# Taking each feed-forward down projection one chunk later

## The chip, the cores and the metric

The kernel runs on one core of one Trainium2 chip. The metric is the device time of one execution in microseconds (us). Three executions of the kernel before took 2207.88, 2215.27 and 2216.32 us; their median, 2215.27 us, is the time before.

Five engines work side by side and wait for each other through semaphores: PE (TensorE, matmuls, with PEld for its weight loads), ACT (ScalarE), DVE (VectorE), POOL (GpSimd, used here mostly to issue DMAs) and SP (SyncE, which issues the other DMAs). Each engine takes its own instructions in order.

## The reference, cut to what matters

A four-layer model on 256 tokens of width 1024, all in 32-bit floats. Each layer is feed-forward block, mixer, feed-forward block, and each of the three is followed by a layer norm over a scaled residual. The mixers are a state-space block (layers 0 and 3) and two kinds of attention (layers 1 and 2). So there are eight feed-forward blocks, all of the same form:

```python
def swiglu(x, w_gate, w_up, w_down):
    return (jax.nn.silu(x @ w_gate) * (x @ w_up)) @ w_down

ff = swiglu(h, ffn_w_gate[layer, 0], ffn_w_up[layer, 0], ffn_w_down[layer, 0])
h = layer_norm(DEEPNORM_ALPHA * h + MACARON_WEIGHT * ff, ln_g[layer, 0], ln_b[layer, 0])
```

The hidden width is 2816, which is 11 chunks of 256 columns.

## The kernel before

**Streams.** The 256 tokens are two tiles of 128 tokens, t = 0 and t = 1. Each is a Python generator (`stream`, and inside it `ffn`, `ssm` or `attn`) that yields whenever it needs the next piece of weights. The loop at the end of `build` advances stream 0 to piece s and then stream 1 to piece s - 2 (`LAG` = 2), so the two streams use the same weights two pieces apart and their matmuls alternate on PE.

**Weights.** All weights are cut on the host into pieces of 128 x 2048 floats (1 MB) in the order in which `ffn`, `ssm` and `attn` ask for them; `pack_ffn` sets that order for a feed-forward block, 33 pieces: 22 of gate and up columns (two per chunk) and 11 of down rows (one per chunk). `load` fetches a piece by a DMA on SP into one of three `raw` buffers, and then splits it in four quarters into a rounded high part `wh` (ACT, L123) and the rest `wl` (DVE, L124), with five buffers of each. `advance` loads two pieces ahead of stream 0 (`PF` = 2); a buffer comes free when stream 1 has used it. Every product is three matmuls (`mm3`, L148 to L150): high by high, high activations by low weights, low activations by high weights. A piece is 12 matmuls of 128 x 512 in either stream.

**A chunk.** `proj512` makes gate and up of chunk c, 256 columns each, in one PSUM bank `gu` from two pieces (24 matmuls). ACT takes the SiLU of the gate half (L269), DVE multiplies it by the up half (L271). The down projection (`down`, into the two banks `acc`) needs the product transposed and split into `ah` and `al`. The transpose does not use PE: `turn_begin` transposes 32 x 32 blocks on DVE (`tb`, L240), POOL writes the result to DRAM (`turn`, L242) and issues four DMAs that read it back in the turned layout (`aT`, L246). `turn_end` splits `aT` into `ah` on ACT and `al` on DVE (both lines 123 and 124, as for weights). The ACT half is held to its place in program order. Three `aT` buffers are there.

**The order before.** In `ffn`, chunk c's gate-up pieces are followed by the down piece of chunk c - 1, whose `turn_end` stands between the two halves of chunk c:

```python
for c in range(NC_F + 1):
    ...
    if half and c:
        acts[c - 1] = turn_end(turns.pop(c - 1))
    ...
    if c > 0:
        w = yield
        down(st, *acts.pop(c - 1), w, c == 1, c == NC_F)
```

In pieces: gate-up 0 (pieces 0 and 1), gate-up 1 (2 and 3), down 0 (4), gate-up 2 (5 and 6), down 1 (7), and so on. Chunk 10, the last, does not go through DRAM: its product is transposed on PE by `act_split` at high priority, after down 9 has been written. The order inside each engine's queue is finally set by the framework's scheduler, which follows the program but may pull work of one stream ahead of the other's.

Of the kernel before, what the change touches and what calls it, by code (L numbers as in the profile page):

```python
# [7 lines left out]
F32 = mybir.dt.float32  # L8
FR = mybir.dt.float32r
BF = mybir.dt.bfloat16  # L10
AF = mybir.ActivationFunctionType
# [9 lines left out]
NC_F = DFF // 256  # L21
# [24 lines left out]
def mixer_of(layer):  # L46
    return ("ssm", "fox", "moba")[layer % 3], layer // 3


def build(tc, x, wst, ln_g, ln_b, sm_dt, sm_rows, sm_conv, sm_nw, fx_f, fx_b, out, plan=None):  # L50
    nc = tc.nc
# [4 lines left out]
    spool = ctx.enter_context(tc.tile_pool(name="s", bufs=2))  # L56
# [13 lines left out]
    def G():  # L70
        return ps_g.tile([128, 512], F32, name="gu")
# [4 lines left out]
    def tmp(cols, tag, bufs, dt=F32):  # L76
        return spool.tile([128, cols], dt, name=tag, tag=tag, bufs=bufs)
# [44 lines left out]
    def split(raw, wh, wl):  # L122
        a = nc.scalar.activation(wh, raw, AF.Copy)  # L123
        return a, nc.vector.tensor_sub(wl, raw, wh.bitcast(F32))  # L124
# [22 lines left out]
    def mm3(o, xh, xl, wh, wl, start, stop):  # L147
        nc.tensor.matmul(o, xh, wh, start=start, stop=False)  # L148
        nc.tensor.matmul(o, xh, wl, start=False, stop=False)  # L149
        nc.tensor.matmul(o, xl, wh, start=False, stop=stop)  # L150
# [4 lines left out]
    def transposes(src, n):  # L155
        tp = T()
        for j in range(n):
            nc.tensor.transpose(tp[:, j * 128:(j + 1) * 128], src[:, j * 128:(j + 1) * 128], ident)  # L158
        return tp
# [43 lines left out]
    def down(st, ah, al, w, first, last):  # L203
        wh, wl = w
        if first:
            st.acc = [ps_a.tile([128, 512], F32, name=f"acc{n}") for n in range(2)]
        for m in range(4):
            kk, n = (m % 2, m // 2) if last else (m // 2, m % 2)
            o = kk * 1024 + n * 512
            mm3(st.acc[n], ah[:, kk], al[:, kk], wh[:, o:o + 512], wl[:, o:o + 512],  # L210
                first and kk == 0, last and kk == 1)

    def proj512(st, ps, half, w):
        wh, wl = w
        for kk in range(4):
            k = half * 4 + kk
            mm3(ps, st.xh[:, k], st.xl[:, k], wh[:, kk * 512:(kk + 1) * 512], wl[:, kk * 512:(kk + 1) * 512],
                k == 0, k == KT - 1)
# [7 lines left out]
    def act_split(src, n):  # L226
        tp = transposes(src, n)
        pairs = []
        for m in range(0, n, 2):
            ah = spool.tile([128, 2, 128], FR, name="ah", bufs=5)  # L230
            al = spool.tile([128, 2, 128], FR, name="al", bufs=5)
            split(tp[:, m * 128:(m + 2) * 128].rearrange("p (a b) -> p a b", a=2), ah, al)
            pairs.append((ah, al))
        return pairs

    def turn_begin(a, n):


        b = spool.tile([128, 4, n, 32], F32, name="tb", bufs=2)
        nc.vector.transpose(b.rearrange("p q k t -> p (q k t)"), a.rearrange("p (k q j) -> p q k j", k=n, q=4))  # L240
        dr = dpool.tile([128, 128 * n], F32, name="turn", bufs=4)
        nc.gpsimd.dma_start(dr, b.rearrange("p q k t -> p (q k t)"))  # L242
        aT = spool.tile([128, 4, n, 32], F32, name="aT", bufs=3)
        dv = dr.rearrange("(i f) (q c) -> q f i c", i=4, q=4)
        for q in range(4):
            nc.gpsimd.dma_start(aT[32 * q:32 * q + 32].rearrange("p i k t -> p i (k t)"), dv[q])  # L246
        return aT

    def turn_end(aT):
        ah = spool.tile([128, 2, 128], FR, name="ah", bufs=5)  # L250
        al = spool.tile([128, 2, 128], FR, name="al", bufs=5)
        v4 = lambda v: v.rearrange("p k (i t) -> p k i t", i=4)
        ins = split(aT.rearrange("p i k t -> p k i t"), v4(ah), v4(al))
        tc.keep_in_program_order(ins[0])
        return ah, al

    def ffn(st, hook):
        acts, turns = {}, {}
        for c in range(NC_F + 1):
            if c < NC_F:  # L260
                gu = G()
                for half in range(2):
                    w = yield
                    if half and c:
                        acts[c - 1] = turn_end(turns.pop(c - 1))
                    proj512(st, gu, half, w)
                with tc.high_priority() if c == NC_F - 1 else nullcontext():
                    sg = tmp(256, "t1", 5)
                    nc.scalar.activation(sg, gu[:, :256], AF.Silu)  # L269
                    a = tmp(256, "t1", 5)  # L270
                    nc.vector.tensor_mul(a, sg, gu[:, 256:])  # L271
                    if c < NC_F - 1:
                        turns[c] = turn_begin(a, 2)
            if c == 4 and hook is not None:
                hook()
            if c > 0:
                w = yield
                down(st, *acts.pop(c - 1), w, c == 1, c == NC_F)
            if c == NC_F - 1:
                with tc.high_priority():  # L280
                    acts[c] = act_split(a, 2)[0]

    def small():
        return tmp(32, "sm", 16)
# [457 lines left out]
    def stream(st):  # L742
        init(st)
        yield
        to_T(st, st.h)
        for n, (kind, l, li) in enumerate(plan):
            w = yield
            if n:
                with tc.high_priority():
                    to_T(st, st.h)  # L750
            if kind == "ffn":
                hook = None
                if st.t == 0 and n + 1 < len(plan) and plan[n + 1][0] == "mix":
                    mk, j = mixer_of(plan[n + 1][1])
                    hook = {"ssm": lambda j=j: ssm_small(j), "fox": lambda j=j: fox_small(j), "moba": consts}[mk]
                body = ffn(st, hook)
                c = 0.5 / ALPHA
            else:
                mk, j = mixer_of(l)
                body = ssm(st, j) if mk == "ssm" else attn(st, mk, j)  # L760
                c = 1.0 / ALPHA
            next(body)
            while True:
                try:
                    body.send(w)
                except StopIteration:
                    break
                w = yield
            layer_norm(st, c, li, n == len(plan) - 1)
            if st.t == 1 and n + 1 < len(plan):  # L770
                ln_weights(plan[n + 1][2])
# [23 lines left out]
    for kind, l, li in plan:  # L795
        n = 3 * NC_F if kind == "ffn" else 28 if mixer_of(l)[0] == "ssm" else 16
# [13 lines left out]
def rows2(a):  # L810

    n = a.shape[0] // 256
    return a.reshape(n, 2, 128, D).transpose(0, 2, 1, 3).reshape(n, 128, 2048)


def cols512(a):

    return list(a.reshape(2, 4, 128, 512).transpose(0, 2, 1, 3).reshape(2, 128, 2048))
# [6 lines left out]
def pack_ffn(g, u, d):  # L825
    P = []
    dn = rows2(d)
    for c in range(NC_F):
        sl = slice(c * 256, c * 256 + 256)
        P += cols512(np.concatenate([g[:, sl], u[:, sl]], axis=1))  # L830
        if c:
            P.append(dn[c - 1])
    P.append(dn[NC_F - 1])
    return P


def pack_ssm(w_in, w_out):
# [34 lines left out]
def layout(I, plan=None):  # L872
# [6 lines left out]
    for kind, l, li in plan:  # L879
        if kind == "ffn":  # L880
            h = 0 if li % 3 == 0 else 1
            P += pack_ffn(I["ffn_w_gate"][l, h], I["ffn_w_up"][l, h], I["ffn_w_down"][l, h])
            continue
        mk, j = mixer_of(l)
        if mk == "ssm":
            P += pack_ssm(I["ssm_w_in"][j], I["ssm_w_out"][j])
        else:
            P += pack_att(I[mk + "_w_in"][j], I[mk + "_w_out"][j])
# [39 lines left out]
```

## Time and profile before

| | |
|---|---|
| profiled execution, its own time | 2211.85 us |
| its span, first to last instruction | 2210.1 us |
| PE busy | 2142.6 us, 97% of the span |
| DVE busy | 1487.4 us, 67% |
| ACT busy | 1126.8 us, 51% |
| POOL busy | 478.2 us, 22% |
| DMA | 438.82 MB, mean 199 GB/s |
| granted TensorE clock, mean | 0.989 |
| feed-forward matmuls, `gu` of 512 columns | 3 x 1536, about 600 us each third |
| `acc` matmuls (feed-forward and mixers) | 3 x 896, about 359 us each third |

Times in the rows are microseconds from the start of the span unless they are marked ns. A row that ends with "[4.83 <-ACT ah L123]" says that the engine was idle for 4.83 us before that instruction and that the `ah` split on ACT, line 123, ended the idle time. Matmuls are pipelined, so their durations overlap; what counts is the distance from one start to the next. In a table of stretches each engine has its busy time and, in brackets, the number of its instructions that touch the stretch; PEclk is the mean clock that was granted to TensorE, 1.00 for full.

### The profile page before, as it was taken

How to read it: one execution, taken by the hardware profiler on the slowest of the kernel's cores; microseconds unless marked ns; L12 is line 12 of the kernel's file. 1: busy time of each engine (PE TensorE's matmuls, PEld its weight loads, DVE VectorE, ACT ScalarE, POOL GpSimd, SP SyncE). 2: the span in 40 equal slices, each digit the busy share in tenths (PEclk: the TensorE clock that was granted, in tenths of full speed). 3: DMA queues.
4: the chain of work that ended last, by engine and by line, in shares of the span. 5: the costliest groups of instructions: out<-in, count | busy, mean ns of one | idle time of the engine just before them, and what ended most of it. 6: DMA issues, size and time to landing. Idle time of an engine off the chain costs nothing.

```text
span 2210.1 us, 29948 instructions
## 1 busy us (share of the span) xinstructions
PE 2142.6 (97%) x10370; PEld 1779.5 (81%) x10370; DVE 1487.4 (67%) x2959; ACT 1126.8 (51%) x2314; POOL 478.2 (22%) x862
## 2 busy tenths in 40 slices
PE   8999999999999999999999999999999999999998
PEld 6888878788878888878878888878878888787887
DVE  5667998765756574656565674655566578998565
ACT  5444776444444445544444455544445447664442
POOL 2331000233133200033223310033323310002232
PEclk9999999999999999999999999999999999999999
DMA  8766554677666743466667764467656765455763
GB/s 290 226 222 200 186 176 154 205 226 223 206 216 224 226 154 115 148 209 225 219 205 226 225 201 133 134 196 228 222 194 226 235 191 191 164 177 194 221 225 104
DMA packets 225928, 438.82 MB, mean 199 GB/s; under 512 B 20464, under 2 KB 20976, under 8 KB 225776
## 3 DMA queue, kind: packets, MB, share of 16 engines
q1 hardware_dynamic: 197616, 394.92, 53.7%
q0 software_dynamic: 28160, 41.99, 6.7%
q8 instruction: 81, 1.33, 0.2%
q14 instruction: 71, 0.58, 0.1%
HBM read 414.74 MB, written 22.09 MB: 198 GB/s over the span
## 4 chain that ended last, share of the span: by engine, by line
PE 85%; DVE 6%; DMA 3%; issue 3%; ACT 1%; POOL 1%; SPq 0%; DVEq 0%; ACTq 0%; POOLq 0%
PE gu L150 14%; PE gu L148 14%; PE gu L149 14%; PE acc L148 9%; PE acc L150 9%; PE acc L149 9%; PE ga L150 3%; PE ga L148 3%; PE ga L149 3%; PE tp L158 2%; DVE wl L124 2%; DMA aT<-turn 2%; PE gu L508 1%; DMA turn<-tb 1%; PE tp L653 1%
## 5 line engine op out<-in xcount | busy, mean ns | idle before, releaser
L124 DVE TENSOR_TENSOR wl<-raw,wh 128x512 fp32r<-128x512 f32 x1408 | 889.2, 683 | 374.7 <-ACT wh L123 373.1
L123 ACT ACTIVATE wh<-raw 128x512 fp32r<-128x512 f32 x1408 | 778.0, 621 | 517.5 <-PE gu L150 244.8
L148 PE MATMUL gu<-wh,xh 128*128 128x512 f32 (+1 forms) x1600 | 619.9, 388 | 7.2 <-ACT t L515 2.7
L150 PE MATMUL gu<-wh,xl 128*128 128x512 f32 (+1 forms) x1600 | 617.4, 386 | 0.9 <-DVE xl L124 0.9
L149 PE MATMUL gu<-wl,xh 128*128 128x512 f32 (+1 forms) x1600 | 617.2, 386 | 0.0
L246 POOL DMA_DIRECT2D aT<-turn x640 | 348.2, 551 | 496.2 <-issue 301.9
L148 PE MATMUL acc<-wh,ah 128*128 128x512 f32 x896 | 359.0, 401 | 34.3 <-ACT ah L123 34.3
L149 PE MATMUL acc<-wl,ah 128*128 128x512 f32 x896 | 358.9, 401 | 0.0
L150 PE MATMUL acc<-wh,al 128*128 128x512 f32 x896 | 358.6, 400 | 0.0
L148 PEld LDWEIGHTS gu<-wh,xh 128*128 128x128 f32 x1600 | 301.1, 188 | 69.9 <-ACT t L515 3.2
L150 PEld LDWEIGHTS gu<-wh,xl 128*128 128x128 f32 x1600 | 301.3, 188 | 62.1 <-DVE xl L124 2.1
L149 PEld LDWEIGHTS gu<-wl,xh 128*128 128x128 f32 x1600 | 301.1, 188 | 60.0 <-issue 0.5
L148 PEld LDWEIGHTS acc<-wh,ah 128*128 128x128 f32 x896 | 172.3, 192 | 72.3 <-ACT ah L123 37.7
L150 PEld LDWEIGHTS acc<-wh,al 128*128 128x128 f32 x896 | 172.4, 192 | 38.8 <-DVE al L124 2.1
L269 ACT ACTIVATE t<-gu 128x256 f32<-128x256 f32 x176 | 67.4, 383 | 266.6 <-PE gu L150 266.2
L149 PEld LDWEIGHTS acc<-wl,ah 128*128 128x128 f32 x896 | 172.3, 192 | 35.5 <-issue 1.0
L271 DVE TENSOR_TENSOR t<-t,gu 128x256 f32<-128x256 f32 x176 | 73.6, 418 | 179.9 <-ACT t L269 179.8
L242 POOL DMA_DIRECT2D turn<-tb x160 | 90.3, 565 | 421.8 <-DVE tb L240 404.6
L148 PE MATMUL ga<-wh,xh 128*128 128x512 f32 (+1 forms) x448 | 158.9, 356 | 1.4 <-ACT xh L123 1.4
L149 PE MATMUL ga<-wl,xh 128*128 128x512 f32 (+1 forms) x448 | 157.7, 352 | 0.0
L150 PE MATMUL ga<-wh,xl 128*128 128x512 f32 (+1 forms) x448 | 156.1, 350 | 0.1
L124 DVE TENSOR_TENSOR al<-aT,ah 128x256 fp32r<-128x256 f32 x160 | 67.1, 419 | 46.1 <-ACT ah L123 46.0
(179 smaller groups left out, 1663.7 us busy)
## 6 DMA issues: line engine op xcount, KB each, us to landing
raw<-in_w_dram SPq DMA_DIRECT2D x351, 1024.0 KB, 5.6
turn<-tb POOLq DMA_DIRECT2D x160, 128.0 KB, 3.1
aT<-turn POOLq DMA_DIRECT2D x640, 32.0 KB, 4.2
mt<-cums SPq DMA_DIRECT2D x32, 256.0 KB, 4.4
gb<-in_ln_g_dram SPq DMA_DIRECT2D x12, 512.0 KB, 4.6
gb<-in_ln_b_dram SPq DMA_DIRECT2D x12, 512.0 KB, 5.9
nw<-in_sm_nw_dram SPq DMA_DIRECT2D x8, 256.0 KB, 5.5
h<-in_x_dram SPq DMA_DIRECT2D x4, 256.0 KB, 4.0
```

The source lines that it names most:

```text
L123: a = nc.scalar.activation(wh, raw, AF.Copy)
L124: return a, nc.vector.tensor_sub(wl, raw, wh.bitcast(F32))
L148: nc.tensor.matmul(o, xh, wh, start=start, stop=False)
L149: nc.tensor.matmul(o, xh, wl, start=False, stop=False)
L150: nc.tensor.matmul(o, xl, wh, start=False, stop=stop)
L158: nc.tensor.transpose(tp[:, j * 128:(j + 1) * 128], src[:, j * 128:(j + 1) * 128], ident)
L242: nc.gpsimd.dma_start(dr, b.rearrange("p q k t -> p (q k t)"))
L246: nc.gpsimd.dma_start(aT[32 * q:32 * q + 32].rearrange("p i k t -> p i (k t)"), dv[q])
L269: nc.scalar.activation(sg, gu[:, :256], AF.Silu)
L271: nc.vector.tensor_mul(a, sg, gu[:, 256:])
L508: nc.tensor.matmul(y[:, c64], mt[h // 4][:, h % 4], xd[:, c64], start=True, stop=True)
L653: nc.tensor.matmul(o, qz[:, h], kt[:, h // 2], start=not begun, stop=True, skip_group_check=True)
```

## The change

The down piece of chunk c - 2 now follows gate-up c, and `turn_end` of chunk c - 2 stands between the halves of chunk c. In pieces: gate-up 0 (0 and 1), gate-up 1 (2 and 3), gate-up 2 (4 and 5), down 0 (6), gate-up 3 (7 and 8), down 1 (9), and so on; at the end of a block down 8, down 9 and down 10 stand in a row, with `turn_end` of chunk 9 before down 8 and `act_split` of chunk 10 after it. `pack_ffn` lays the weights out in the same order. `aT` has five buffers.

```diff
-        aT = spool.tile([128, 4, n, 32], F32, name="aT", bufs=3)
+        aT = spool.tile([128, 4, n, 32], F32, name="aT", bufs=5)
...
-        for c in range(NC_F + 1):
...
+        for c in range(NC_F):
+            gu = G()
+            for half in range(2):
+                w = yield
+                if half and c > 1:
+                    acts[c - 2] = turn_end(turns.pop(c - 2))
+                proj512(st, gu, half, w)
+            tail = c == NC_F - 1
+            with tc.high_priority() if tail else nullcontext():
...
+                if not tail:
+                    turns[c] = turn_begin(a, 2)
             if c == 4 and hook is not None:
                 hook()
-            if c > 0:
-                w = yield
-                down(st, *acts.pop(c - 1), w, c == 1, c == NC_F)
-            if c == NC_F - 1:
-                with tc.high_priority():
-                    acts[c] = act_split(a, 2)[0]
+            for d in range(c - 2, NC_F if tail else c - 1):
+                if d >= 0:
+                    w = yield
+                    if d == NC_F - 3:
+                        acts[d + 1] = turn_end(turns.pop(d + 1))
+                    down(st, *acts.pop(d), w, d == 0, d == NC_F - 1)
+                    if d == NC_F - 3:
+                        with tc.high_priority():
+                            acts[NC_F - 1] = act_split(a, 2)[0]
...
-        if c:
-            P.append(dn[c - 1])
-    P.append(dn[NC_F - 1])
-    return P
+        if c > 1:
+            P.append(dn[c - 2])
+    return P + list(dn[NC_F - 2:])
```

What this does to the queues is shown at the start of the third feed-forward block (the second of layer 0). Names carry buffer generations here: `gu_5746` and `gu_5743` are the bank of chunk 1 of stream 1, `gu_5717` is chunk 2 of stream 0, `acc0` and `acc1` are the two down banks, `wh_5629` is piece 4 of the block and `wh_5550` piece 2.

PE before, where the block's first down projection stands:

```order
L150 MATMUL gu_5746<-wh_5550,xl1_5652 128x512
L148 MATMUL gu_5746<-wh_5550,xh1_5651 128x512
L149 MATMUL gu_5746<-wl_5551,xh1_5651 128x512
L148 MATMUL acc0_5759<-wh_5629,ah_5692 128x512
L149 MATMUL acc0_5759<-wl_5630,ah_5692 128x512
L150 MATMUL acc0_5759<-wh_5629,al_5693 128x512
```

PE now, around stream 0's first down projection (`wh_5746` is now piece 6, `wh_5591` piece 3):

```order
L148 MATMUL gu_5743<-wh_5591,xh1_5651 128x512
L149 MATMUL gu_5743<-wl_5592,xh1_5651 128x512
L150 MATMUL gu_5743<-wh_5591,xl1_5652 128x512
L148 MATMUL acc0_5859<-wh_5746,ah_5792 128x512
L149 MATMUL acc0_5859<-wl_5747,ah_5792 128x512
L150 MATMUL acc0_5859<-wh_5746,al_5793 128x512
```

Before, 58 matmuls of 512 columns and 8 transposes stand between the last gate-up matmul of stream 0's chunk 0 and its first down matmul; now it is 96 and 8. Over the eight blocks the distance grows by 35 to 46 such matmuls.

ACT before, at the same place (`ah_5692` is stream 0's chunk 0; `wh_5749` and `wh_5788` are pieces 6 and 7):

```order
L123 ACTIVATE wh_5682<-raw_5680 128x512 x4
L269 ACTIVATE t1_5708<-gu_5626 128x256
L269 ACTIVATE t1_5733<-gu_5667 128x256
L123 ACTIVATE wh_5749<-raw_5747 128x512 x3
L123 ACTIVATE ah_5692<-aT_5621 128x256
L123 ACTIVATE wh_5749<-raw_5747 128x512
L123 ACTIVATE wh_5788<-raw_5786 128x512 x4
```

ACT now (`ah_5792` is stream 0's chunk 0; `wh_5746` and `wh_5782` are pieces 6 and 7):

```order
L123 ACTIVATE wh_5682<-raw_5680 128x512 x4
L270 ACTIVATE t1_5704<-gu_5626 128x256
L270 ACTIVATE t1_5730<-gu_5667 128x256
L123 ACTIVATE wh_5746<-raw_5744 128x512 x4
L123 ACTIVATE wh_5782<-raw_5780 128x512 x4
L123 ACTIVATE ah_5792<-aT_5621 128x256
L270 ACTIVATE t1_5808<-gu_5717 128x256
L270 ACTIVATE t1_5833<-gu_5743 128x256
```

The first `ah` of the block stood after three quarters of piece 6; it now stands after all of pieces 6 and 7. The sequences of POOL and SP keep their order, but for two neighbours that change places in the first block on POOL and three small loads for the mixers that move by one place on SP. No engine has more or fewer instructions.

More of the change, by code (lines that the diff above doesn't have):

```diff
@@ L258, in ffn @@
         acts, turns = {}, {}
-        for c in range(NC_F + 1):
-            if c < NC_F:
-                gu = G()
-                for half in range(2):
-                    w = yield
[L264 to L273, printed above, removed]
+        for c in range(NC_F):
[7 more added lines that the diff above has]
+            with tc.high_priority() if tail else nullcontext():
+                sg = tmp(256, "t1", 5)
+                nc.scalar.activation(sg, gu[:, :256], AF.Silu)
+                a = tmp(256, "t1", 5)
+                nc.vector.tensor_mul(a, sg, gu[:, 256:])
+                if not tail:
+                    turns[c] = turn_begin(a, 2)
             if c == 4 and hook is not None:
                 hook()
-            if c > 0:
-                w = yield
-                down(st, *acts.pop(c - 1), w, c == 1, c == NC_F)
-            if c == NC_F - 1:
-                with tc.high_priority():
-                    acts[c] = act_split(a, 2)[0]
+            for d in range(c - 2, NC_F if tail else c - 1):
[7 more added lines that the diff above has]
+                            acts[NC_F - 1] = act_split(a, 2)[0]
     def small():
```

## The prediction, made before the changed kernel ran

> **What bounds the kernel now.** I read the engines' shares first, then who waited for whom on the engine that leads, then the instructions around one such wait, and last stretches of equal length with and without it.
>
> ```profile
> PE 2142.6 (97%) x10370; PEld 1779.5 (81%) x10370; DVE 1487.4 (67%) x2959; ACT 1126.8 (51%) x2314; POOL 478.2 (22%) x862
> PE acc L148 <- ACT ah L123: 34.3, 8, 4.9
> PE tp L158 <- DMA h<-in_x_dram: 6.4, 2, 3.7
> L149 PE MATMUL acc<-wl,ah 128*128 128x512 f32 x896 | 358.9, 401 | 0.0
> ```
>
> PE is busy for 97% of the span, so only what PE does or waits for can move the end. Its largest wait by far is that of `acc` for the `ah` split: 34.3 us in 8 waits, none over 4.9 us. There are eight feed-forward blocks, and `acc` has 896 matmuls in each third, so this is one wait per block and not a steady loss. The next in size is the input at the start, which the change leaves alone. One of the eight, in the third block, matmul by matmul:
>
> ```profile
> 612.10 0.39 PE L148 MATMUL gu<-wh,xh 128*128 128x512 f32 x1
> 612.33 0.39 PE L149 MATMUL gu<-wl,xh 128*128 128x512 f32 x1
> 617.54 0.79 PE L148 MATMUL acc<-wh,ah 128*128 128x512 f32 x1 [4.83 <-ACT ah L123]
> 618.14 0.63 PE L149 MATMUL acc<-wl,ah 128*128 128x512 f32 x1
> 618.56 0.63 PE L150 MATMUL acc<-wh,al 128*128 128x512 f32 x1
> ```
>
> Ahead of the wait a matmul starts 0.23 us after the last; behind it the distance is 0.42 us (618.14 to 618.56), nearly twice, and one takes 0.63 us instead of 0.39. The wait costs more than its idle time. How much more is read from stretches of 20 us on PE, one around each of the eight waits and two without any (640 and 50):
>
> ```profile
> core 0: us, PE busy (x), PEclk, DMA share, GB/s
> 30.00:50.00 20.00, 16.00 (x64) 0.91 0.74 247
> 50.00:70.00 20.00, 20.00 (x90) 1.00 0.72 237
> 424.00:444.00 20.00, 16.00 (x65) 0.91 0.61 190
> 612.00:632.00 20.00, 15.17 (x56) 0.83 0.56 183
> 640.00:660.00 20.00, 20.00 (x90) 1.00 0.70 233
> 942.00:962.00 20.00, 15.83 (x64) 0.91 0.55 188
> 1132.00:1152.00 20.00, 15.98 (x61) 0.83 0.61 193
> 1449.00:1469.00 20.00, 15.73 (x59) 0.83 0.55 169
> 1640.00:1660.00 20.00, 15.08 (x57) 0.83 0.57 187
> 2035.00:2055.00 20.00, 15.91 (x63) 0.91 0.58 179
> ```
>
> A stretch without a wait holds 90 matmuls at clock 1.00. A matmul counts when any of its 0.39 us lies inside, so 90 stand for 20.39 us, 0.2266 us each. The eight stretches with a wait hold 64 + 65 + 56 + 64 + 61 + 59 + 57 + 63 = 489 instead of 720, and their clock is 0.83 to 0.91. The 231 missing matmuls are 231 x 0.2266 = **52.3 us**: 34.3 us of waiting, and 18.0 us for matmuls that ran at a lowered clock after it (with the pipeline's refilling).
>
> [...]
>
> **The change, part by part.** *Removed: the distance that was too short.* `ah` of chunk 0 needs the SiLU, the product, the turn through DRAM and the split:
>
> ```profile
> 598.70 0.39 ACT L269 ACTIVATE t<-gu 128x256 f32<-128x256 f32 x1 [3.49 <-PE gu L150]
> 604.30 0.60 POOL L242 DMA_DIRECT2D turn<-tb  x1 [6.88 <-DVE tb L240]
> 610.07 2.18 POOL L246 DMA_DIRECT2D aT<-turn  x4 [5.16 <-issue]
> 617.08 0.42 ACT L123 ACTIVATE ah<-aT 128x256 fp32r<-128x256 f32 x1 [4.88 <-DMA aT<-turn]
> ```
>
> From the SiLU at 598.70 to `ah` at 617.08 pass 18.4 us. In the old order 58 matmuls of 512 columns and 8 transposes fill that time in this block, which at 0.2266 us is 13.1 us and a little. The new order puts 38 more there (96), 8.6 us, against a wait of 4.83 us. Over the eight blocks the added distance is 35 to 46 matmuls, 7.9 to 10.4 us; the longest wait is 4.9 us, so by the data every block has at least 3 us to spare. Stream 1's first down projection goes from 60 to 108 matmuls behind its chunk; it waits for nothing in either.
>
> *Moved: `ah` in ACT's queue.* It now stands behind all of pieces 6 and 7 of the weights. This can eat the spare time, since the split of piece 7 must wait until stream 1 has used piece 2. These rows show such a split after the same release:
>
> ```profile
> 623.54 2.19 ACT L123 ACTIVATE wh<-raw 128x512 fp32r<-128x512 f32 x4 [5.53 <-issue]
> 624.21 2.50 DVE L124 TENSOR_TENSOR wl<-raw,wh 128x512 fp32r<-128x512 f32 x4 [5.05 <-ACT wh L123]
> 626.62 0.42 DVE L124 TENSOR_TENSOR al<-aT,ah 128x256 fp32r<-128x256 f32 x1
> ```
>
> From the start of `wh` on ACT to the end of `wl` on DVE 3.2 us pass (623.54 to 626.71), and `al` adds 0.4: 3.6 us at most. In the new order stream 0's piece 5 and stream 1's piece 3 follow that release, 24 matmuls, 5.4 us, before the first `acc`; `al` is first needed two matmuls later. That leaves about 2 us. Behind `ah` in the queue stand the two SiLUs, then piece 8; none is due on PE for another 12 matmuls. So the wait should go in all eight blocks, and with it the low clock: 52.3 us.
>
> *Moved: three gate-up chunks at the start of a block.* A `gu` bank must have been read by ACT and DVE before the next chunk but one may use it. PE already shows that wait, and the reads themselves are short:
>
> ```profile
> 422.18 0.50 PE L148 MATMUL gu<-wh,xh 128*128 128x512 f32 x1 [0.50 <-DVE t L271]
> L269 ACT ACTIVATE t<-gu 128x256 f32<-128x256 f32 x176 | 67.4, 383 | 266.6 <-PE gu L150 266.2
> L271 DVE TENSOR_TENSOR t<-t,gu 128x256 f32<-128x256 f32 x176 | 73.6, 418 | 179.9 <-ACT t L269 179.8
> ```
>
> 0.38 + 0.42 us against 12 matmuls (2.7 us) of cover. Two such close follow-ups per block at 0.5 us each bound the loss at 16 x 0.5 = 8 us; below it is nothing. Most follow-ups of this kind pass without a wait, so I take 2 us.
>
> *The end of a block.* Down 8, 9 and 10 in a row put 12 more matmuls of either stream between chunk 10's product and down 10. PE shows no wait there now, so this is worth nothing; at worst the early `act_split` of chunk 10 breaks a run of matmuls as it did before.
>
> *Buffers and DMAs.* The number of instructions is the same on every engine. Weights, turns and read-backs are as many and as large as before, and POOL and SP keep their sequences. Two more `aT` buffers hold the chunk that is under way longer; POOL's issue of `aT` waits for one only behind the landing of `turn`. Nothing.
>
> *Sum.* -52.3 + 2 = -50.3 us. The profiled execution took 2211.85 us (its span is 2210.1), which is 3.4 us under the median of 2215.27. So the profiled time should be 2161.6 us, and the median **2165 us**.
>
> **The rivals.** *A part of the wait stays.* The turn is not of fixed length:
>
> ```profile
> DMA to landing us min/median/max: 1.9/4.2/6.7
> turn<-tb POOLq DMA_DIRECT2D x160, 128.0 KB, 3.1
> raw<-in_w_dram SPq DMA_DIRECT2D x351, 1024.0 KB, 5.6
> ```
>
> The read-back lands after 1.9 to 6.7 us, and piece 7 may arrive late at the start of a block. With 1.5 us left in each block, 12 us come back, and 30 us if the clock still falls (18 us): 2177 to 2195 us. Against it stand the 3 us and 2 us above. [...]
>
> *The wait moves in full.* If POOL's serial turns were the limit, a later use would only shift the wait to the next down projection, and the time stays at 2215 us. Against it: PE waits for `ah` 8 times and not 160, so the turns keep pace once a block runs.
>
> *The weights become the bound, and it is slower.* In the stretches with a wait DMA is busy 0.55 to 0.61 of the time in seven of eight, in the two others 0.70 and 0.72: the waits give SP's transfers a rest. Without them all 264 feed-forward pieces must come one per 24 matmuls, 5.44 us. A `raw` buffer is taken for 5.6 us until landing and some 3.2 us for the splits, 8.8 us, and there are three: one piece per 2.9 us. It turns into a loss when a piece takes 0.2 us more than 5.44 (52.3 / 264), that is when landing takes 3 x 5.64 - 3.2 = 13.7 us. At 14 us a piece costs 5.73 us, 77 us over all, and the kernel ends at 2215 - 50 + 77 = 2242 us. The stretches at 640 and 50 speak against it: 20 us busy in 20 us at the full rate of weights.
>
> **How the numbers follow.** All eight waits go: 0.80, 2165 us, by itself 2158 to 2171 (0 to 8 us at the banks, and the spread of the runs). A part stays: 0.11, 2177 to 2195. It moves in full: 0.05. Slower: 0.04. The range of 2154 to 2184 us holds the first case and half of the second. About 0.5%, 11 us, is what a measurement of this kernel can tell from no change; the first two cases lie beyond it: faster 0.91, same 0.05, slower 0.04.
>
> **What would show it.** Right: the wait of PE's `acc` for `ah` falls from 34.3 us to under 3; stretches of 20 us at the start of each block hold close to 90 matmuls at clock 1.00; the mean clock rises from 0.989 to over 0.995; PE's busy time falls by some 18 us although it has the same matmuls. ACT's idle time before `ah` with the DMA of `aT` as releaser goes to nearly nothing. It is wrong if waits of `gu` for the product on DVE come to over 8 us, if `acc` waits for `al` on DVE instead of `ah`, if PE waits for `wl`, or if the clock falls at other places.

## The result, and the profile after

| | before | after |
|---|---|---|
| median | 2213.53 us (2207.88 to 2216.32) | 2158.63 us (2158.25 to 2159.97) |
| profiled execution | 2211.85 us | 2158.25 us |
| its span | 2210.1 us | 2156.1 us |
| mean granted clock | 0.989 | 0.999 |

The ratio is 0.9756, with a 95% interval of 0.9735 to 0.9777: 2.4% faster. The median of before is taken over its first three executions and one more beside the changed kernel.

The shares of the engines, with the largest group of down matmuls, a DMA row and a group of ACT, after:

```profile
PE 2122.0 (98%) x10370; PEld 1768.2 (82%) x10370; DVE 1486.4 (69%) x2959; ACT 1125.5 (52%) x2314; POOL 477.6 (22%) x862
L148 PE MATMUL acc<-wh,ah 128*128 128x512 f32 x896 | 351.5, 393 | 0.0
L123 ACT ACTIVATE ah<-aT 128x256 fp32r<-128x256 f32 x160 | 64.4, 402 | 0.0
raw<-in_w_dram SPq DMA_DIRECT2D x351, 1024.0 KB, 5.6
```

The number behind the last bar is the idle time ahead of a group. For `acc` by `ah` it is 0.0 now; the wait of 34.3 us that led the list before is gone. ACT no longer stands idle ahead of its `ah` group; before, it did for 51.1 us, until `aT` had landed:

```profile
L123 ACT ACTIVATE ah<-aT 128x256 fp32r<-128x256 f32 x160 | 64.6, 404 | 51.1 <-DMA aT<-turn 51.1
```

PE has its 10370 matmuls as before and is busy for 20.6 us less (2142.6 to 2122.0). The weights land in 5.6 us as they did.

The waits of PE after (engine and line, what it waited for: us in all, times, longest):

```profile
PE tp L158 <- DMA h<-in_x_dram: 3.7, 1, 3.7
PE tp L158 <- DVE wl L124: 3.6, 1, 3.6
...
PE gu L148 <- DVE t L272: 1.2, 3, 0.6
```

What is largest now is the input at the start and one transpose beside it. The wait of a `gu` bank for the product on DVE is 1.2 us in three places; before it was 1.4 us in three places.

Stretches of 20 us after, at the places where the eight blocks now take their first down projections:

```profile
core 0: us, PE busy (x), PEclk, DMA share, GB/s
30.00:50.00 20.00, 20.00 (x90) 1.00 0.99 317
420.00:440.00 20.00, 20.00 (x90) 1.00 0.81 259
600.00:620.00 20.00, 20.00 (x90) 1.00 0.77 242
920.00:940.00 20.00, 20.00 (x89) 1.00 0.72 229
1105.00:1125.00 20.00, 20.00 (x90) 1.00 0.83 265
1415.00:1435.00 20.00, 20.00 (x90) 1.00 0.81 242
1600.00:1620.00 20.00, 20.00 (x90) 1.00 0.83 264
1985.00:2005.00 20.00, 20.00 (x90) 1.00 0.90 274
```

All hold 89 or 90 matmuls at clock 1.00, where the stretches with a wait held 56 to 65 at 0.83 to 0.91. DMA reaches 0.99 of its time in the first of them, and PE does not wait there.

**Where the time went.** The span fell by 54.0 us: PE is busy for 20.6 us less and idle for 33.4 us less. The idle part is the 34.3 us of waits (other waits differ by a microsecond). The busy part is the same matmuls at the full clock: 18.0 us were counted for the eight places in the prediction. A further low stretch of before lies outside the feed-forward blocks, in the first state-space mixer:

```profile
290.00:295.00 5.00, 4.60 (x23) 0.73 0.29 99
```

After has none there: its clock is 1.00 from 270 to 300 us. It is worth up to 1.4 us (0.27 of 5 us). Whether that is the change's doing or chance stays open.

### The profile page after: what moved, and what is told of

The parts are those of the page before. It is cut to its first block, busy times and chain, and to the rows that moved or that the text cites. A ratio compares the mean times of both kernels' runs of the same rounds, so it can differ in the third digit from the quotient of the medians.

```text
span 2156.1 us, 29943 instructions
## 1 busy us (share of the span) xinstructions
PE 2122.0 (98%) x10370; PEld 1768.2 (82%) x10370; DVE 1486.4 (69%) x2959; ACT 1125.5 (52%) x2314; POOL 477.6 (22%) x862
## 4 chain that ended last, share of the span: by engine, by line
PE 93%; DVE 3%; ACT 1%; DMA 1%; issue 0%; POOL 0%; SPq 0%; DVEq 0%; ACTq 0%
PE gu L148 15%; PE gu L150 15%; PE gu L149 15%; PE acc L150 9%; PE acc L148 9%; PE acc L149 9%; PE ga L150 4%; PE ga L149 4%; PE ga L148 4%; PE tp L158 3%; PE gu L512 1%; DMA raw<-in_w_dram 1%; PE tp L657 1%; DVE wl L124 1%; DVE mt L502 1%
## 5 line engine op out<-in xcount | busy, mean ns | idle before, releaser
L150 PE MATMUL acc<-wh,al 128*128 128x512 f32 x896 | 353.5, 395 | 0.0
L149 PE MATMUL acc<-wl,ah 128*128 128x512 f32 x896 | 352.5, 393 | 0.0
L148 PE MATMUL acc<-wh,ah 128*128 128x512 f32 x896 | 351.5, 393 | 0.0
L190 POOL TENSOR_TENSOR rstd<-ve,mhalf 128x1 f32<-128x1 f32 x24 | 22.6, 942 | 369.9 <-DVE ve L188 369.9
```

The source lines that it names most:

```text
L190: nc.gpsimd.tensor_tensor(rstd, ve, mhalf, op=ALU.pow)
```

## The experiments

The theory: chunk 0's product comes back from its turn through DRAM too late for the first down projection of each block; the wait costs its own length and then lowers the clock, and the change removes both by putting more matmuls in between. The rivals: the buffers did it; the longer distance pays at every chunk and not only at the first; it is the clock and not the wait, or the wait and not the clock, that costs. None of the eight kernels leaves out a part of the computation; two add useless matmuls and two add transfers. "Before" in the ratios is the kernel before beside the run: 2211.75 us in the median for the first three kernels below and the one with 28 useless matmuls, 2213.42 us for the other four. Beside the changed kernel it was 2213.53 us, so a difference from the changed kernel is good to some 2 us.

### Only the first down projection later

The list of pieces is gate-up 0, 1, 2, down 0, down 1, gate-up 3, down 2, gate-up 4, and so on: chunk 0 gets the longer distance, every later chunk the old one. `aT` has five buffers.

```diff
+def ffn_order():
     P = []
+    for c in range(NC_F):
+        P += [("g", c, 0), ("g", c, 1)]
+        P += [("d", d, 0) for d in ([] if c < 2 else [0, 1] if c == 2 else [c - 1])]
+    return P + [("d", NC_F - 1, 0)]
...
-        aT = spool.tile([128, 4, n, 32], F32, name="aT", bufs=3)
+        aT = spool.tile([128, 4, n, 32], F32, name="aT", bufs=5)
```

> Only the first down projection of a block is delayed (gate-up 0, 1, 2, down 0, down 1, gate-up 3, down 2, ...); from chunk 3 on, and at the end of the block, the order is that of before. Theory (only the first distance was too short; everything from chunk 1 on had cover enough): all of the change's gain, 2157 to 2163 us, and no wait of PE's acc for ah. Rival (the longer distance all through a block is worth something, by keeping ACT, POOL and DMA off PE's path): a part of the gain is missing, 2170 us or more, with waits of acc for ah or al after the first chunk.

Measured: 2162.43 us (2159.51 to 2166.53), ratio 0.9775 (0.9758 to 0.9792): 49.3 us under the kernel before beside it, and 3.8 us above the changed kernel. The time lies in the range of the theory, but "no wait of PE's acc for ah" does not hold in the profiled execution. What stays is seen first in PE's waits and then in the two places, in the fifth block:

```profile
PE acc L148 <- ACT ah L123: 4.2, 2, 2.1
...
1123.62 0.50 PE L148 MATMUL acc<-wh,ah 128*128 128x512 f32 x1 [2.09 <-ACT ah L123]
1139.64 0.50 PE L148 MATMUL acc<-wh,ah 128*128 128x512 f32 x1 [2.12 <-ACT ah L123]
```

The timeline around them shows stream 0's 12 matmuls of down 0 from 1115.93 without a wait, then 12 of stream 1's gate-up, and then this wait: it is down 1, of stream 0 and, 16 us later, of stream 1. Nearly all of the gain is the first down projection. The second one, which has the old distance here and no longer has a wait ahead of it that would give its own turn time, is on the edge. The four executions fall in two pairs, 2159.5 and 2159.7, 2165.1 and 2166.5, and the profiled one is the slowest. So the longer distance behind the first chunk is worth 3.8 us between the medians, but only 1 us by the faster pair; that the two waits are what parts the pairs is not shown.

### Only the five buffers

```diff
-        aT = spool.tile([128, 4, n, 32], F32, name="aT", bufs=3)
+        aT = spool.tile([128, 4, n, 32], F32, name="aT", bufs=5)
```

> The order of before, with five aT buffers instead of three. Theory (the buffers are room only): as before, 2208 to 2217 us, with the wait of acc for ah still near 34 us. Rival (POOL's issue of the read-back waited for a free aT buffer, and that was part of the delay): the wait shrinks, and the time falls by 5 us or more.

Measured: 2212.12 us (2208.7 to 2216.21), ratio 1.0001 (0.9991 to 1.0011).

```profile
PE acc L148 <- ACT ah L123: 31.2, 8, 4.5
```

All eight waits are there. In the old order the buffers do nothing by themselves; whether the new order needs all five was not tried.

### The transposed chunk 0 without the trip

The old order, but chunk 0 of either stream is transposed on PE and split there, as chunk 10 is, instead of going through DRAM.

```diff
-                    if half and c:
+                    if half and c > 1:
                         acts[c - 1] = turn_end(turns.pop(c - 1))
...
-                    if c < NC_F - 1:
+                    if 0 < c < NC_F - 1:
                         turns[c] = turn_begin(a, 2)
+                if c == 0:
+                    acts[0] = act_split(a, 2)[0]
```

> The order of before, but chunk 0 of either stream is transposed on PE (as chunk 10 is) and does not go through DRAM. Theory (the turn through DRAM is what was late at the first down projection): the waits of acc for ah go without any change of order. The price is 2 transposes of 128 columns per stream and block, 32 more instructions at some 0.1 to 0.4 us each, 3 to 13 us: 2162 to 2175 us. Rival (something else at the start of a block holds the first down projection, such as the layer norm's work on DVE ahead of the product): waits of acc or of the transposes stay, 2185 us or more.

Measured: 2163.42 us (2162.77 to 2164.84), ratio 0.9785 (0.977 to 0.9799), clock 0.998. In its groups the down matmuls stand with no idle time:

```profile
L148 PE MATMUL acc<-wh,ah 128*128 128x512 f32 x896 | 351.8, 393 | 0.0
```

With the order as it was and only the trip of chunk 0 taken out, the waits are gone too, and the low clock behind them. It is the trip that was late, not something else in the old order. The median is 4.8 us above that of the changed kernel. The profiles, 7.0 us apart in their spans (2163.1 against 2156.1), show where such a price comes from: PE is busy for 9.0 us more (2131.0 against 2122.0), 7.4 us of it in the row of the transposes, which are 32 more (x320 and 57.1 us against x288 and 49.7 us).

### Half of the added distance

Down c - 2 between the two halves of gate-up c: about half as many matmuls more as in the change.

```diff
+    for c in range(NC_F):
+        P += [("g", c, 0)] + [("d", c - 2, 0)] * (c > 1) + [("g", c, 1)]
+    return P + [("d", NC_F - 2, 0), ("d", NC_F - 1, 0)]
```

> Half of the delay: the down piece of chunk c - 2 stands between the two gate-up pieces of chunk c. Counted over the order of instructions, the distance from stream 0's chunk 0 to its first down matmul is 15.9 to 17.2 us, against 16.5 to 19.1 us that were needed in the kernel before. Theory (the wait is need minus distance, block by block): waits of acc for ah of 1.2 to 2.1 us in six blocks and none in two, some 10 us in all, each too short to lower the clock: 2165 to 2171 us, mean clock 0.997 or more. Rival A (any wait at this place costs the clock as well): some 2 us more per wait, 2177 to 2183 us. Rival B (need follows the order and not the clock of the turn): no wait at all, 2157 to 2161 us.

Measured: 2171.8 us (2170.58 to 2173.64), ratio 0.9812 (0.9796 to 0.9828).

```profile
PE acc L148 <- ACT ah L123: 8.3, 6, 2.5
```

Waits are left in six blocks and gone in two, and all are shorter than the old ones: 8.3 us in all where 31 to 34 were. So the wait shrinks with the matmuls put in between. The time came out just above the range put down for it, and "each too short to lower the clock" was wrong for one wait: behind 1.85 us of idle time the clock fell to 0.50 for 3.41 us (last section). The time is 13.2 us above the changed kernel: 8.3 us of waits, an estimated 1.6 us for that low stretch (16 - 9 matmuls of 0.2266 us each), and some 3 us that stay open.

### A longer trip in the new order

The changed kernel, with stream 0's chunk 0 copied once more from DRAM to DRAM before it is read back, and in a second kernel twice.

```diff
-    def turn_begin(a, n):
+    def turn_begin(a, n, trips=0):
...
         nc.gpsimd.dma_start(dr, b.rearrange("p q k t -> p (q k t)"))
+        for _ in range(trips):
+            again = dpool.tile([128, 128 * n], F32, name="again", bufs=4)
+            nc.gpsimd.dma_start(again, dr)
+            dr = again
...
-                    turns[c] = turn_begin(a, 2)
+                    turns[c] = turn_begin(a, 2, 1 if c == 0 and st.t == 0 else 0)
```

> The changed kernel, with the product of stream 0's chunk 0 sent through DRAM once more (one DMA of 128 KB from DRAM to DRAM, before the read-back; nothing left out). It lengthens the turn of that chunk alone, by an issue of some 0.6 us and a landing of 3 to 6 us. By the distances in the new order (21.3 to 22.6 us) and the need of before (16.5 to 19.1 us) 3.5 to 6.1 us are to spare. Theory (the change buys 3.5 to 6 us of room in each block): waits of 0 to 3 us come back in some blocks, without a lowered clock: 2158 to 2178 us. [...]

Measured with one more trip: 2167.74 us (2165.79 to 2170.72), ratio 0.9795 (0.978 to 0.9809). PE's waits and the DMA issue (number, size, median us to landing):

```profile
PE acc L148 <- ACT ah L123: 6.1, 5, 3.1
...
again<-turn POOLq DMA_DIRECT2D x8, 128.0 KB, 5.3
```

The trip is 5.3 us longer, and of that only 6.1 us over eight blocks (0.8 us a block on average) come out as waits. Three blocks show none. The longest is 3.1 us. In the first block the clock was 0.50 from 44.50 to 47.90, with 9 matmuls there; over the whole span its mean is 0.998.

> The same with two more trips, 7 to 13 us longer. Theory: the room is used up in every block, waits of 2 to 9 us, above some 3 us with a lowered clock after them: 2185 to 2250 us, and the wait grows from the run with one trip by the length of the second trip. Rival (the turn does not set the first down projection in the new order; the split's place behind pieces 6 and 7 does): waits stay under 2 us, below 2175 us.

Measured with two: 2218.4 us (2212.46 to 2224.72), ratio 1.0024 (1.0009 to 1.004).

```profile
PE acc L148 <- ACT ah L123: 38.3, 8, 6.9
...
again<-turn POOLq DMA_DIRECT2D x8, 128.0 KB, 5.1
again<-again POOLq DMA_DIRECT2D x8, 128.0 KB, 4.1
```

The second trip lands in 4.1 us, and the waits grow by 32.2 us, 4.0 us on average over the eight blocks: once the room is used, a longer trip comes out on PE nearly in full. Two trips make 9.2 us, and the waits are 38.3 / 8 = 4.8 us on average, so the new order had some 4.4 us to spare on average (by the median landing times; each trip adds an issue on POOL beside it). Where the wait was longest it had less: 9.2 - 6.9 = 2.3 us, and 5.3 - 3.1 = 2.2 us by the kernel with one trip. The whole gain is gone. The profiled execution, the fastest of ten, is 54.2 us longer than that of the changed kernel, 38.3 us of waits and 15.9 us more, at a mean clock of 0.990. That is close to the split of before, 34.3 and 18.0. A lowered clock followed all eight waits of before, 4.00 to 4.92 us long; the "some 3 us" in the expectation was my estimate and too high, since 1.85 us of idle time was enough at half the distance (last section).

### The wait filled with useless work

The old order, with 28 useless matmuls of 128 x 512 ahead of stream 0's first down projection in each block, meant to keep the clock up through the same wait.

```diff
                 w = yield
+                if c == 1 and st.t == 0:
+                    idle = T()
+                    for _ in range(28):
+                        nc.tensor.matmul(idle, st.xh[:, 0], w[0][:, 0:512], start=True, stop=True)
                 down(st, *acts.pop(c - 1), w, c == 1, c == NC_F)
```

> The order of before; ahead of stream 0's first down projection in each block PE does 28 matmuls of 512 columns whose result nobody reads (extra work, nothing left out). They take 28 x 0.2266 = 6.3 us, and by the order of instructions the distance from the chunk's last gate-up matmul to the first down matmul becomes 16.8 to 18.1 us against 16.5 to 19.1 us that were needed. Theory (18 of the 52 us are the lowered clock after an idle PE): the wait is filled with work of no use, so the 34 us stay spent, but the clock stays up: some 2195 to 2201 us, mean clock 0.998, left-over waits of about 1 us in five or six blocks without a lowered clock. Rival (the matmuls after the wait are slow for another reason, such as the split of the weights or the down banks): 2213 us or more, and 0.42 us between the starts of the first acc matmuls as before.

Measured: 2215.99 us (2213.28 to 2220.48), ratio 1.0022 (1.0013 to 1.0032), where I expected a gain of the clock's share. Its groups and waits:

```profile
L281 PE MATMUL tp<-wh,xh 128*128 128x512 f32 x224 | 52.1, 389 | 0.0
...
PE acc L148 <- ACT ah L123: 6.1, 5, 2.2
```

The mean clock stayed at 0.997. But the scheduler had put 11 matmuls of stream 1 behind the filling, which had covered a part of the trip before, so the 28 went in place of useful work as well as of the wait. 224 x 0.2266 = 50.8 us of filling and 6.1 us of waits, on top of 2158.6 us, make 2215.5; 2215.99 was measured. The profiled execution, from which the waits are read, took 2220.48 us, and its mean clock of 0.997, against 0.999 after, is left out of the sum. It closes on the median partly by luck, and the kernel does not price the clock by itself.

The second such kernel keeps those matmuls ahead: stream 1 goes first at that step, and 18 useless matmuls remain.

```diff
+            if kind == "ffn" and s == 4:
+                advance(1, base + s - LAG)
...
-            if s >= LAG:
+            if s >= LAG and not (kind == "ffn" and s == 4):
                 advance(1, base + s - LAG)
...
+                    for _ in range(18):
```

> The order of before, with stream 1's piece 2 placed ahead of stream 0's first down projection, where the scheduler had put 11 of its 12 matmuls in any case, and 18 matmuls of 512 columns without use behind it (extra work, nothing left out). They take 18 x 0.2266 = 4.1 us, about as long as PE was idle. In the first run with such a filling the scheduler had moved stream 1's matmuls behind the wait, so that the sum there is filling (50.8 us) plus left-over waits (6 us) in place of the 52.3 us of before: it showed that the clock stays up, not what this is worth. Theory (18 us of the loss are the lowered clock after PE was idle): 8 x 4.1 = 32.6 us of filling and 2 to 5 us of left-over waits stand in place of the 52.3 us: 2193 to 2199 us. Rival (the first matmuls behind the wait are slow for another reason): 2208 us or more, with 0.42 us between their starts.

Measured: 2202.36 us (2200.44 to 2205.03), ratio 0.9951 (0.9936 to 0.9965), some 3 us above the range that I had written down.

```profile
L281 PE MATMUL tp<-wh,xh 128*128 128x512 f32 x144 | 33.9, 389 | 0.0
...
PE acc L148 <- ACT ah L123: 3.1, 4, 1.9
PE acc L150 <- DVE al L124: 1.8, 5, 0.5
```

In the third block, where the kernel before took 0.42 us from start to start behind the wait, the filling runs up to the first down projection and the distance is 0.23 us:

```profile
613.36 4.24 PE L281 MATMUL tp<-wh,xh 128*128 128x512 f32 x18
...
617.74 0.40 PE L149 MATMUL acc<-wl,ah 128*128 128x512 f32 x1
617.97 0.39 PE L150 MATMUL acc<-wh,al 128*128 128x512 f32 x1
```

So the first down matmuls are not slow for a reason of their own, as the rival had it. PE spends 144 x 0.2266 = 32.6 us on useless work and 4.9 us in waits, 37.5 us, where it had waited for 34.3 us before. It computes nothing more than before, yet the kernel is 11.1 us faster (7.7 to 14.2), at a clock of 0.998. That is the low clock's price, apart from the wait: 11.1 us, or 14.3 us when the 3.2 us more of filling are taken off. The 18.0 us counted in the prediction held the pipeline's refilling too, as it said; and one wait of 1.91 us in this kernel still lowered the clock (last section). Some 2 us of the difference stay open. By the sum used for the first filling, 2158.6 + 32.6 + 4.9 = 2196.1 us, the kernel should have been 6.3 us faster; the low stretch behind the wait of 1.91 us is an estimated 1.4 us of this (10 matmuls instead of 16, 0.2266 us each), the rest is not explained.

## Why the prediction was right

The forecast was 2165 us in a range of 2154 to 2184; 2158.63 us was measured. The case that I had put first came true, "all eight waits go".

- *What bounds the kernel.* PE, and on it the eight waits of `acc`. Right: taking away only the trip of chunk 0, or only its short distance, gives 48.3 and 49.3 us.
- *52.3 us for the waits and what follows them.* Right in size: 34.3 us of waiting went to nothing, and the clock rose from 0.989 to 0.999. PE busy fell by 20.6 us where "some 18" was said; up to 1.4 us of the 20.6 is the low stretch in the mixer.
- *The distance, "at least 3 us to spare".* Right on average, 4.4 us from the two longer trips, but not in every block: the least was some 2.2 us. The wait went there all the same. Half of the distance left waits in six blocks of eight.
- *`ah` in ACT's queue, "about 2 us" left.* Right, and here the trip is no longer what comes last. In the third block, after, on ACT, DVE and PE (it is the first block of layer 1, not the second of layer 0, as the text on the change calls it):

```profile
585.99 0.39 ACT L270 ACTIVATE t<-gu 128x256 f32<-128x256 f32 x1 [3.24 <-PE gu L150]
...
603.29 2.20 ACT L123 ACTIVATE wh<-raw 128x512 fp32r<-128x512 f32 x4 [3.04 <-issue]
605.39 0.40 ACT L123 ACTIVATE ah<-aT 128x256 fp32r<-128x256 f32 x1
```
```profile
606.37 0.42 DVE L124 TENSOR_TENSOR al<-aT,ah 128x256 fp32r<-128x256 f32 x1
```
```profile
608.48 0.39 PE L148 MATMUL acc<-wh,ah 128*128 128x512 f32 x1
...
608.93 0.39 PE L150 MATMUL acc<-wh,al 128*128 128x512 f32 x1
```

  `ah` starts right behind the split of piece 7, without idle time of its own, 19.4 us after the SiLU (18.4 us before). It is done at 605.79, and PE asks for it at 608.48: 2.7 us. `al` is done at 606.79 and is asked for at 608.93: 2.1 us.
- *The `gu` banks, 0 to 8 us, 2 taken.* The term was sized too large. The follow-ups cost nothing (1.2 us after, 1.4 us before). This is 2 of the 3.4 us by which the profiled time was predicted too long (2161.6 against 2158.25); the rest is of the size of the low stretch in the mixer.
- *Median against profile.* I had added 3.4 us because before's profiled execution was so much under its median. The changed kernel's profiled execution is its fastest and only 0.4 us under its median. This made up half of the 6.4 us by which the median was missed.
- *The slower rival*, in which the weights become the bound, had a sound premise (the waits gave the transfers a rest) and no effect: DMA is busy 0.72 to 0.99 of the stretches, a piece still lands in 5.6 us, PE waits for no piece once the first has come.
- *The rival with a part of the wait left* took 1.5 us in each block, at 12 us, or 30 us if the clock falls. Both kinds of left-over wait are in the runs: 1.60 us of idle time was followed by a clock of 1.00, and 1.85 us by one of 0.50. The last section has the rows.

## What to carry to other kernels

When one engine bounds a kernel and waits once per block, look for the first item of the block: there the pipeline has nothing old to work on, and one more item in flight only there brings nearly all of the gain. Count the cover in instructions of the bounding engine from the moment the long trip starts, and read how far the clock falls from stretches around the wait: here a wait cost on average about half as much again as its idle time (18.0 us beside 34.3 us). Room of a few microseconds was enough (4.4 us on average), and it was used up as soon as the trip grew by twice as much (9.2 us).

## What was not expected of the hardware

Idle times of 1.85 and 1.91 us were followed by a lowered clock, where the shortest wait of before was 4.00 us. In the trace of before, the clock was 0.50 in ten pieces of the span: nine are 3.413 or 6.827 us long, the tenth runs to the end of the span, and all of them start whole numbers of 3.413 us apart. The rows below are stretches of that length and, in each kernel, whole numbers of it apart. In the kernel at half the distance:

```profile
core 0: us, PE busy (x), PEclk, DMA share, GB/s
422.73:426.14 3.41, 1.56 (x7) 1.00 0.87 318
426.14:429.55 3.41, 3.41 (x9) 0.50 0.33 69
429.55:432.97 3.42, 3.42 (x16) 1.00 0.92 312
607.03:610.44 3.41, 1.81 (x9) 1.00 0.88 264
610.44:613.85 3.41, 2.53 (x11) 1.00 0.62 216
```

From 422.73 PE is idle for 1.85 us of the stretch, and the whole next stretch runs at a clock of 0.50, with 9 matmuls instead of 16. That is an estimated 7 x 0.2266 = 1.6 us beside the wait. From 607.03 PE is idle for 2.48 us in all, more than there, but 1.60 us of it lies in one stretch and 0.88 us in the next, and both are at 1.00. The kernel with two more trips, the one with 18 useless matmuls, and the one with only the first down projection later:

```profile
625.06:628.47 3.41, 1.71 (x8) 1.00 0.82 252
628.47:631.89 3.42, 3.04 (x13) 1.00 0.67 198
952.74:956.15 3.41, 0.86 (x5) 1.00 0.93 311
956.15:959.56 3.41, 3.41 (x9) 0.50 0.28 69
```
```profile
1460.55:1463.97 3.42, 1.51 (x7) 1.00 0.01 1
1463.97:1467.38 3.41, 3.41 (x10) 0.50 0.15 46
```
```profile
1122.13:1125.54 3.41, 1.92 (x8) 1.00 0.77 295
1125.54:1128.96 3.42, 3.42 (x16) 1.00 0.23 75
1135.78:1139.20 3.42, 1.75 (x8) 1.00 0.80 276
1139.20:1142.61 3.41, 2.97 (x13) 1.00 0.08 19
```

In these rows 1.49, 1.60, 1.67 and 1.70 us of idle time in a stretch were followed by a clock of 1.00, and 1.85, 1.91 and 2.55 us by one of 0.50. In the kernel before, cut in the same way, stretches at full clock with up to 1.49 us of idle time were followed by another at 1.00 and those with 2.17 us or more by one at 0.50, with two exceptions: 2.76 us from 5.59 to 9.01, where PE waits for the input, was followed by 1.00, and 1.03 us in a mixer by 0.50 (below). In the kernel before, a wait could cost two stretches:

```profile
613.17:616.58 3.41, 0.00 (x0) 1.00 0.71 240
616.58:619.99 3.41, 2.44 (x6) 0.50 0.09 23
619.99:623.41 3.42, 3.42 (x10) 0.50 0.79 269
623.41:626.82 3.41, 3.41 (x17) 1.00 0.31 96
```

The stretch in which the wait ended was busy for 2.44 of 3.41 us only, and it was low and so was the next; after a fully busy one the clock came back. In this execution the low stretches with up to 0.57 us of idle time were followed by the full clock, and those with 0.97 us or more by another low one. Four of the eight stretches quoted in the prediction have a mean clock of 0.91 and four of 0.83, which in 20 us is one low stretch and two: twelve, and 18.0 us over twelve are 1.5 us each. So waits of nearly the same length cost different amounts: the one of 4.00 us that ends at 429.42 comes with one low stretch, the one of 4.02 us that ends at 1137.26 with two.

The low stretch in the state-space mixer of before (from 292.31 us) came with less idle time than these, 1.03 us, followed by 16 matmuls of only 64 columns in 2.00 us; whether such short matmuls count for less, no run here separates, and what lowered the clock there stays open.
